# v's split first, k's hi halves ahead, and lasting k_lo buffers in a stick-breaking attention block

## The chip, the cores and the metric

The kernel runs on one core of one Trainium2 chip. The metric is the device time of one execution in microseconds (us). Everything is computed in fp32: a number is held as two parts, hi (the value rounded to fp32r) and lo (the rest), and a product of two such numbers takes three matmuls on TensorE (PE): hi by hi, lo by hi and hi by lo. The other engines are ScalarE (ACT), VectorE (DVE), GpSimd (POOL) and the queue that issues most DMAs (SP). Each engine works through its own list of instructions in order, and the engines wait for each other by semaphores.

## What is computed

One layer of a decoder trunk over 1024 tokens and a model width of 1024. The part that matters here is the attention: q, k and v come from one projection, q and k are normalised per head, and the weights are made by stick breaking.

```python
hn = rms_norm(h, norm1_g[i])
proj = hn @ w_in[i]
a_b, a_c, a_h, q, k, v, c_u, c_v = jnp.split(proj, split_idx, axis=-1)
...
q = rms_norm(q.reshape(bsz, s_len, ATTN_HEADS, HEAD_DIM), q_norm_g[i])
k = rms_norm(k.reshape(bsz, s_len, ATTN_HEADS, HEAD_DIM), k_norm_g[i])
y_b = stick_breaking_attention(q, k, v).reshape(bsz, s_len, ATTN_W)
...
h = h + jnp.concatenate([y_a, y_b, y_c], axis=-1) @ w_out[i]
f = jnp.square(jax.nn.relu(rms_norm(h, norm2_g[i]) @ w_ff1[i]))
h = h + f @ w_ff2[i]
gate = jax.nn.sigmoid(rms_norm(h, norm3_g[i]) @ w_ple_gate[i])
h = h + gate * (p[i] @ w_ple_proj[i])
```

In the attention, with z the scaled product of a query and a key (8 heads of 64), a weight is sigmoid(z) times the product of sigmoid(-z) over the later keys before the query, and the output is the weighted sum of v.

## The kernel before

The program runs in stages: the gating heads' projections and the first pair's q, k, v (up to about 100 us of the trace); attention, woven with the projections of the next pair of heads and at last with the convolution (to about 345 us); the output projection, the MLP and the last gate (to the end).

**The projection.** `project(pr)` (L343) makes q, k and v of one pair of heads, for four pairs. It goes over eight blocks of 128 tokens. A block is 24 matmuls (L165 to L167) into one PSUM bank `qkv_ps` of 128 x 384: q and k of two heads in columns 0 to 255, v in columns 256 to 383. Two banks (`ps_mm`, two buffers) serve in turn, so block b+2 can't begin before block b's bank has been read for the last time. I count the blocks through the four pairs, 0 to 31.

What reads a bank, in the order of the code: ACT squares q and k (`qk_sq`, L371), DVE sums the squares (`ss`, L374), POOL raises them to -1/2 (`rs`, L174), DVE multiplies q and k by that (`qk`, L379), and then v is split: ACT writes its hi part (`V`, L141) and DVE its lo part (`V`, L142). Where the reader of a bank changes from one engine to another, the built program has the second engine wait for the first.

**The turned bank.** After every second block `turn_qk` (L390) transposes q and k of two blocks on PE into a bank `qk_tr`, and for each of the two heads of the pair (64 partitions each) writes five parts from it: ACT q's hi (`QS`, L402) and k's hi (`KH`, L403) in the head's own rows, DVE q's lo (`QS`, L404, in the other rows) and k's lo (`KL`, L406), and ACT k's hi once more in the other rows (`KH`, L408). The other rows of `KL` have to be zero, and POOL clears them (L359) when a tile is taken, twice for each half of the tokens: 16 times.

**The attention.** `stick` (L427) makes z (L439, L441, L445) in two banks; ACT writes two sigmoids of it (`rem`, L446, and `wt`, L447); DVE runs the product over the later keys (L451, a scan), and POOL or DVE multiplies (L454). `gather` (L461) transposes the weights (`w_tr`, L476), splits them (`wT_hi` on ACT, `wT_lo` on DVE) and multiplies by V (`av`, L494).

**What sets the order.** `weave` (L267) alternates between attention and projection by units of PE work. Within that, a scheduler orders the instructions of each engine when the program is built, from costs of its own; the order on each engine is then fixed. Tiles of the tag `slot` come from one pool of 56, and `load_w` (L145) splits the next pair's weights (`whi` on ACT, `wlo` on DVE or POOL) in the same stretch.

## Time and profile before

| | us |
|---|---|
| time, median of 3 runs | 1219.47 |
| lowest and highest run | 1216.49, 1220.53 |
| the profiled execution's own time | 1217.19 |
| its span in the trace | 1215.2 |

The profile lists busy time by engine; a view by windows gives the busy time of each engine in a stretch of the span; a view of waits sums, for each engine and line, how long the engine stood idle and which instruction of another engine ended that; the timeline lists instructions in order of time, with the idle time just before one in brackets. PE is matmul and PEld the load of weights beside it. A matmul's listed time overlaps that of its neighbours, so the distance between two starts, not the listed time, is what it takes of PE.

### The profile page before, as it was taken

The page shows a single profiled execution, that of the slowest core. Times are in us where ns is not written, and L with a number is a line of the kernel's source. Part 1 is how long each engine was busy: PE and PEld are TensorE (multiplying, and loading weights), DVE is VectorE, ACT ScalarE, POOL GpSimd, SP SyncE. Part 2 cuts the span into 40 slices and gives each one's busy share as a digit, 9 for nine tenths or more (in the row PEclk, how much of TensorE's full clock was granted, in tenths as well). Part 3 has the DMA queues.
Part 4 walks back from the last instruction along what each step waited for, and adds up shares of the span by engine and source line. Part 5 has one row for each costly group of instructions (what it writes and reads, how often), then busy time and mean ns, then how long its engine had stood idle before and what let it go on. Part 6 is the DMA issues. An engine that isn't in the chain of part 4 may idle for free.

```text
span 1215.2 us, 17769 instructions
## 1 busy us (share of the span) xinstructions
PE 1188.7 (98%) x5852; PEld 1015.5 (84%) x5852; DVE 885.7 (73%) x1302; ACT 641.6 (53%) x1284; POOL 400.5 (33%) x408
## 2 busy tenths in 40 slices
PE   8999999999999999999999999999999999999997
PEld 7899999898878888888888888888888888888886
DVE  7846888888787757877877777787665557753597
ACT  7737777777654355743334343355443444546542
POOL 2324456465342312124553544421023301013412
PEclk9999999999999999999999999999999999999999
DMA  9703359898653786779989989778889985654857
GB/s 300 239 18 102 115 175 278 233 197 160 145 116 79 166 286 194 207 194 266 258 242 271 239 246 264 210 255 273 320 248 314 278 264 170 216 165 108 185 158 208
DMA packets 127964, 254.04 MB, mean 209 GB/s; under 512 B 14496, under 2 KB 22432, under 8 KB 127168
## 3 DMA queue, kind: packets, MB, share of 16 engines
q1 hardware_dynamic: 94992, 168.08, 41.7%
q0 software_dynamic: 27664, 57.05, 25.3%
q10 hardware_dynamic: 5216, 27.79, 6.3%
q8 instruction: 46, 0.75, 0.3%
q14 instruction: 46, 0.38, 0.1%
HBM read 192.30 MB, written 92.80 MB: 235 GB/s over the span
## 4 chain that ended last, share of the span: by engine, by line
PE 84%; DVE 6%; DMA 3%; ACT 3%; issue 2%; POOL 1%; ACTq 0%; SPq 0%; DVEq 0%; POOLq 0%
PE f_ps L811 25%; PE d_ps L811 25%; PE g_ps L811 6%; PE qkv_ps L165 3%; PE qkv_ps L167 3%; PE qkv_ps L166 3%; PE av L494 2%; PE w_tr L476 2%; DVE rem L451 2%; PE vu_ps L167 1%; PE vu_ps L165 1%; PE vu_ps L166 1%; PE o_ps L167 1%; PE o_ps L165 1%; PE o_ps L166 1%
## 5 line engine op out<-in xcount | busy, mean ns | idle before, releaser
L139 DVE TENSOR_TENSOR w_lo<-raw,w_hi 128x512 fp32r<-128x512 f32 x280 | 241.4, 865 | 87.0 <-ACT w_hi L138 85.1
L138 ACT CAST w_hi<-raw 128x512 fp32r<-128x512 f32 x280 | 171.9, 619 | 231.5 <-PE d_ps L811 114.0
L811 PE MATMUL f_ps<-hn_hi,w_hi 128*128 128x512 f32 x448 | 175.2, 392 | 0.0
L811 PE MATMUL f_ps<-hn_hi,w_lo 128*128 128x512 f32 x448 | 174.8, 391 | 0.0
L811 PE MATMUL f_ps<-hn_lo,w_hi 128*128 128x512 f32 x448 | 174.8, 390 | 0.0
L811 PE MATMUL d_ps<-f_hi,w_hi 128*128 128x512 f32 x448 | 174.8, 390 | 0.0
L811 PE MATMUL d_ps<-f_hi,w_lo 128*128 128x512 f32 x448 | 174.3, 389 | 0.0
L811 PE MATMUL d_ps<-f_lo,w_hi 128*128 128x512 f32 x448 | 174.3, 389 | 0.0
L451 DVE TENSOR_TENSOR_SCAN rem<-rem 128x128 f32<-128x128 f32 (+3 forms) x64 | 87.6, 1376 | 19.5 <-ACT rem L446 18.8
L811 PEld LDWEIGHTS f_ps<-hn_lo,w_hi 128*128 128x128 f32 x448 | 84.5, 189 | 17.9 <-issue 0.2
L811 PEld LDWEIGHTS f_ps<-hn_hi,w_hi 128*128 128x128 f32 x448 | 84.5, 189 | 17.9 <-issue 0.2
L811 PEld LDWEIGHTS f_ps<-hn_hi,w_lo 128*128 128x128 f32 x448 | 84.4, 188 | 17.6
L811 PEld LDWEIGHTS d_ps<-f_lo,w_hi 128*128 128x128 f32 x448 | 84.1, 188 | 17.6 <-issue 0.2
L811 PEld LDWEIGHTS d_ps<-f_hi,w_lo 128*128 128x128 f32 x448 | 84.1, 188 | 17.6
L811 PEld LDWEIGHTS d_ps<-f_hi,w_hi 128*128 128x128 f32 x448 | 84.1, 188 | 17.6 <-issue 0.2
L165 PE MATMUL qkv_ps<-whi,xn_hi 128*128 128x384 f32 x256 | 89.6, 350 | 6.8 <-DVE V L142 6.8
L166 PE MATMUL qkv_ps<-wlo,xn_hi 128*128 128x384 f32 x256 | 86.7, 339 | 0.0
L167 PE MATMUL qkv_ps<-whi,xn_lo 128*128 128x384 f32 x256 | 86.6, 338 | 0.0
L139 DVE TENSOR_TENSOR f_lo<-raw,f_hi 128x512 fp32r<-128x512 f32 x112 | 78.1, 728 | 10.1 <-ACT f_hi L138 9.9
L138 ACT CAST f_hi<-raw 128x512 fp32r<-128x512 f32 x112 | 67.1, 620 | 26.0 <-DMA raw<-f_dram 20.9
L797 POOL TENSOR_TENSOR S<-S,sq 128x512 f32<-128x512 f32 x19 | 25.6, 1345 | 160.2 <-ACT sq L873 160.2
L174 POOL TENSOR_TENSOR rs<-ss,mhalf 128x4 f32<-128x4 f32 x32 | 47.5, 1484 | 68.1 <-DVE ss L374 67.3
(247 smaller groups left out, 2707.9 us busy)
## 6 DMA issues: line engine op xcount, KB each, us to landing
raw<-in_w_ff SPq DMA_DIRECT2D x148, 256.0 KB, 4.1
raw<-f_dram SPq DMA_DIRECT2D x112, 256.0 KB, 5.1
raw<-w_sums SPq DMA_DIRECT2D x64, 256.0 KB, 3.7
f_dram<-f SPq DMA_DIRECT2D x48, 256.0 KB, 4.1
f_dram<-t SPq DMA_DIRECT2D x48, 256.0 KB, 3.7
w_sums<-in_w_ff POOLq DMA_DIRECT2D x8, 1024.0 KB, 12.2
w_sums<-w_sums POOLq DMA_DIRECT2D x8, 1024.0 KB, 12.4
raw<-in_w_out SPq DMA_DIRECT2D x28, 256.0 KB, 3.7
```

What stands on the lines that cost most here:

```text
L138: last_hi[0] = nc.scalar.copy(hi, src)
L139: low.tensor_tensor(out=lo, in0=src, in1=hi, op=ALU.subtract)
L165: nc.tensor.matmul(ps, lh, rh, start=first and i == 0, stop=False)
L166: nc.tensor.matmul(ps, lh, rl, start=False, stop=False)
L167: done = nc.tensor.matmul(ps, ll, rh, start=False, stop=last and i == len(terms) - 1)
L174: last_power[0] = nc.gpsimd.tensor_tensor(out=out, in0=in_, in1=mhalf[:, :n], op=ALU.pow)
L451: nc.vector.tensor_tensor_scan(out=back, data0=back, data1=back, initial=1.0, op0=ALU.mult, op1=ALU.bypass)
L476: nc.tensor.transpose(tr[:, n:n + P], wts[i][:, kb * P:(kb + 1) * P], ident)
L494: nc.tensor.matmul(av[:, first * P:], lhs, part[:, o:o + m], start=kb == 0 and part is hi, stop=kb == 2 * g + 1 and part is lo)
L797: return eng.tensor_tensor(out=out, in0=x, in1=y, op=ALU.add)
L811: done = nc.tensor.matmul(bank, l, r, start=first and k == 0 and i == 0, stop=k == len(b) - 1 and i == 2, skip_group_check=True)
```

## The change

The diff has three parts. In `project`, the split of v stands ahead of the squares instead of behind the product `qk`, so a bank is read by ACT (V hi), DVE (V lo), ACT (`qk_sq`), [DVE, POOL,] DVE (`qk`), and `qk` is the last reader instead of V lo. In `turn_qk`, ACT writes k's hi into the own and then the other rows right away, and DVE's two follow, so that ACT's three parts of a head stand together. And k's lo parts lie in lasting tiles, three for the first head of a pair and four for the second, whose other rows are cleared once: 7 clears instead of 16.

```diff
+    k_lo = [[None] * (3 + hh) for hh in range(2)]
+
+    def k_lo_tile(hh, i):
+
+        if k_lo[hh][i] is None:
+            t = k_lo[hh][i] = slot("k_lo", F32R)
+            nc.gpsimd.memset(t[(hi_p, lo_p)[hh]].bitcast(F32), 0.0)
+        return k_lo[hh][i]
+
     def project(pr):
...
             if t % 4 == 0:
-                for hh, other in enumerate((hi_p, lo_p)):
-                    KL[hh][th] = slot("KL", F32R)
-                    nc.gpsimd.memset(KL[hh][th][other].bitcast(F32), 0.0)
                 for hh in range(2):
+                    KL[hh][th] = k_lo_tile(hh, (2 * pr + th) % (3 + hh))
                     QS[hh][th] = slot("QS", F32R)
                     KH[hh][th] = slot("KH", F32R)
             ps = bank(ps_mm, "qkv_ps")[:, :384]
...
                 yield 18
+            if t % 2 == 0:
+                V[t // 2] = slot("V", F32R, (P, 2, 2, 2, HD))
+            v = V[t // 2][:, t % 2]
+            split(ps[:, 256:].rearrange("p (h d) -> p h d", d=HD), v[:, :, 0], v[:, :, 1], scale=r1[t])
 
             sq = half_tmp("qk_sq", (P, 4, HD + 1))
...
                 in1=rs.unsqueeze(2).broadcast_to([P, 4, HD]), op=ALU.mult)
-            if t % 2 == 0:
-                V[t // 2] = slot("V", F32R, (P, 2, 2, 2, HD))
-            v = V[t // 2][:, t % 2]
-            split(ps[:, 256:].rearrange("p (h d) -> p h d", d=HD), v[:, :, 0], v[:, :, 1], scale=r1[t])
...
             nc.scalar.activation(QS[hh][th][own, ws], q, AF.Copy, scale=gq[own])
-            nc.scalar.activation(KH[hh][th][own, ws], k, AF.Copy, scale=gk[own])
+            for part in (own, other):
+                nc.scalar.activation(KH[hh][th][part, ws], k, AF.Copy, scale=gk[own])
             nc.vector.scalar_tensor_tensor(out=QS[hh][th][other, ws], in0=q, scalar=gq[own],
                                            in1=QS[hh][th][own, ws], op0=ALU.mult, op1=ALU.subtract)
             nc.vector.scalar_tensor_tensor(out=KL[hh][th][own, ws], in0=k, scalar=gk[own],
                                            in1=KH[hh][th][own, ws], op0=ALU.mult, op1=ALU.subtract)
-            nc.scalar.activation(KH[hh][th][other, ws], k, AF.Copy, scale=gk[own])
```

The scheduler orders everything anew from the first of these instructions on; from the output projection on, the orders of before and of the change agree but for small exchanges.

The first place is on ACT at the end of the first pair. `qkv_ps_1251` is the bank of block 6, `qkv_ps_1323` that of block 7, and `z_1486` and `z_1492` are products that PE makes behind block 7. Before, the squares of block 6 stand ahead of the sigmoids of an earlier z, and the last reader that ACT gives (V hi) follows the turned bank's parts:

```order
L371 ACTIVATE qk_sq_1311<-qkv_ps_1251 128x4x64
L446 ACTIVATE rem_1373<-z_1375 128x384
...
L408 ACTIVATE KH_1161<-qk_tr_1296,c_gk 64x256
L402 ACTIVATE QS_1162<-qk_tr_1296,c_gq 64x256
L403 ACTIVATE KH_1163<-qk_tr_1296,c_gk 64x256
L141 ACTIVATE V_1320<-qkv_ps_1251,r_731 128x2x64
L138 CAST whi_1415<-stage_1413 128x384
L371 ACTIVATE qk_sq_1348<-qkv_ps_1323 128x4x64
```

With the change the same stretch of ACT reads:

```order
L409 ACTIVATE QS_1162<-qk_tr_1296,c_gq 64x256
L411 ACTIVATE KH_1163<-qk_tr_1296,c_gk 64x256 x2
L141 ACTIVATE V_1311<-qkv_ps_1251,r_731 128x2x64
L138 CAST whi_1409<-stage_1407 128x384
L141 ACTIVATE V_1311<-qkv_ps_1323,r_731 128x2x64
L138 CAST whi_1415<-stage_1413 128x384
L453 ACTIVATE rem_1484<-z_1492 128x512
L453 ACTIVATE rem_1484<-z_1486 128x128
L382 ACTIVATE qk_sq_1314<-qkv_ps_1251 128x4x64
L138 CAST whi_1421<-stage_1419 128x384
L382 ACTIVATE qk_sq_1350<-qkv_ps_1323 128x4x64
```

The squares of block 6 have moved from ahead of the turned bank's parts to behind the V of block 7 and the sigmoids of two products that PE makes after block 7.

On DVE behind that, with the change, the product `qk` of block 6 (the bank's last reader) stands behind these rows; `rem_1484` is the scan over the two sigmoids above, and the `wlo` are weights of the next pair:

```order
L458 SCALAR_TENSOR_TENSOR rem_1484<-rem_1484 128x640
L385 TENSOR_REDUCE ss_1317<-qk_sq_1314 128x4
L385 TENSOR_REDUCE ss_1353<-qk_sq_1350 128x4
L139 TENSOR_TENSOR wlo_1428<-stage_1425,whi_1427 128x384
L139 TENSOR_TENSOR wlo_2251<-stage_2248,whi_2250 128x384
L390 TENSOR_TENSOR qk_1321<-qkv_ps_1251,rs_1319 128x256
```

Before, the scan `rem_1484` stood behind both readers of block 6's bank; now it stands ahead of the sum of its squares.

The second place is on DVE in the third pair, for the bank of block 18 (`qkv_ps_2505` before). Before, from the sum of squares to the last reader, V lo:

```order
L374 TENSOR_REDUCE ss_2603<-qk_sq_2600 128x4
...
L451 SCALAR_TENSOR_TENSOR rem_2512<-rem_2512 128x1024
L454 TENSOR_TENSOR wt_2513<-wt_2513,rem_2512 128x1023
L379 TENSOR_TENSOR qk_2607<-qkv_ps_2505,rs_2605 128x256
...
L451 SCALAR_TENSOR_TENSOR rem_2621<-rem_2621 128x896
...
L142 SCALAR_TENSOR_TENSOR V_2609<-qkv_ps_2505,r_569,V_2609 128x2x64
```

With the change, where that bank is `qkv_ps_2499` and block 19's is `qkv_ps_2606`:

```order
L142 SCALAR_TENSOR_TENSOR V_2594<-qkv_ps_2499,r_569,V_2594 128x2x64
L142 SCALAR_TENSOR_TENSOR V_2594<-qkv_ps_2606,r_569,V_2594 128x2x64
L139 TENSOR_TENSOR wT_lo_2688<-w_tr_2682,wT_hi_2687 128x512
L458 SCALAR_TENSOR_TENSOR rem_2751<-rem_2751 128x640
L385 TENSOR_REDUCE ss_2600<-qk_sq_2597 128x4
L139 TENSOR_TENSOR wT_lo_2721<-w_tr_2716,wT_hi_2720 128x384
L385 TENSOR_REDUCE ss_2696<-qk_sq_2693 128x4
L458 SCALAR_TENSOR_TENSOR rem_2772<-rem_2772 128x768
L461 TENSOR_TENSOR wt_2773<-wt_2773,rem_2772 128x767
L390 TENSOR_TENSOR qk_2604<-qkv_ps_2499,rs_2602 128x256
```

Here too the sum of squares of the earlier block has moved behind a reader of the later block's bank, and two scans stand between V lo and the last reader.

## The prediction

> **What bounds the kernel now.** I read the page's busy times first, then windows by stage, then the waits of PE, then the timeline where PE waited longest.

> ```profile
> span 1215.2 us, 17769 instructions
> PE 1188.7 (98%) x5852; PEld 1015.5 (84%) x5852; DVE 885.7 (73%) x1302; ACT 641.6 (53%) x1284; POOL 400.5 (33%) x408
> ```

> PE is busy for 98% of the span, so a change to ACT, DVE and POOL alone can win at most what PE idles, and can lose by making it idle more. The windows, with the columns PE, PEld, DVE, ACT and POOL busy, tell where that is:

> ```profile
> 120.00:190.00 70.00, 68.81 (x455) 66.44 (x455) 60.41 (x90) 53.48 (x140) 36.07 (x34) 1.00 0.54 156
> 190.00:255.00 65.00, 61.27 (x405) 58.12 (x405) 55.77 (x86) 49.36 (x126) 36.97 (x33) 1.00 0.91 240
> 255.00:320.00 65.00, 61.58 (x400) 58.33 (x399) 56.40 (x88) 48.01 (x123) 33.15 (x32) 1.00 0.81 157
> 320.00:350.00 30.00, 26.93 (x138) 21.99 (x137) 18.87 (x25) 17.90 (x42) 8.72 (x9) 0.94 0.80 170
> ```

> From 120 to 320 us, where projection and attention are woven, PE idles 200 - 191.66 = 8.3 us, and from 320 to 350, where only the convolution is left to fill, 3.1. DVE is at 86% in the three windows to 320 (172.58 of 200) and ACT at 75% (150.85): with in-order lists there is little room behind a late instruction. The two longest sums among PE's waits from 80 to 350 us (us in total, times, longest):

> ```profile
> PE qkv_ps L165 <- DVE V L142: 6.8, 6, 2.5
> PE z L439 <- ACT wt L447: 2.7, 4, 1.0
> ```

> More than half of the idle time is six waits of a projection block for its bank, each ended by the split of v on DVE, the bank's last reader; the rest, 8.3 + 3.1 - 6.8 = 4.6 us at least, is above all attention waiting for ACT or DVE, as the z of the second row. The three longest of the six, at block 8, block 20 and block 28 (the column in brackets is the idle time):

> ```profile
> 118.64 0.44 PE L165 MATMUL qkv_ps<-whi,xn_hi 128*128 128x384 f32 x1 [1.20 <-DVE V L142]
> 215.12 0.44 PE L165 MATMUL qkv_ps<-whi,xn_hi 128*128 128x384 f32 x1 [1.61 <-DVE V L142]
> 282.67 0.44 PE L165 MATMUL qkv_ps<-whi,xn_hi 128*128 128x384 f32 x1 [2.54 <-DVE V L142]
> ```

> The other three make 6.8 - 5.35 = 1.45 us. So the bank's chain of readers is the place where this change decides.

> **The change part by part.** *V first.* The readers of a bank and their lengths:

> ```profile
> L371 ACT ACTIVATE qk_sq<-qkv_ps 128x256 f32<-128x256 f32 x32 | 12.6, 394 | 9.0 <-PE qkv_ps L167 8.6
> L374 DVE TENSOR_REDUCE ss<-qk_sq 128x4 f32<-128x260 f32 x32 | 13.2, 412 | 2.3 <-ACT qk_sq L371 2.0
> L174 POOL TENSOR_TENSOR rs<-ss,mhalf x32: 999/1048/3186, 82.5 to 316.9; 128x4 f32<-128x4 f32 x32
> L379 DVE TENSOR_TENSOR qk<-qkv_ps,rs 128x256 f32<-128x256 f32 x32 | 13.3, 417 | 12.2 <-POOL rs L174 12.1
> L141 ACT ACTIVATE V<-qkv_ps,r 128x128 fp32r<-128x128 f32 x32 | 11.8, 370 | 21.3 <-DVE qk L379 20.9
> L142 DVE SCALAR_TENSOR_TENSOR V<-qkv_ps,r,V 128x128 fp32r<-128x128 f32 x32 | 11.0, 343 | 2.9 <-ACT V L141 2.6
> ```

> Before, these run in this order, with five changes of engine: 0.39 + 0.41 + 1.05 + 0.42 + 0.37 + 0.34 = 2.98 us. The change puts the last two first; the sum is the same 2.98 us, and the changes of engine are again five (ACT, DVE, ACT, DVE, POOL, DVE). A bank isn't freed earlier by itself. What changes is who stands idle: ACT no longer idles 20.9 us behind `qk`; it now waits for V lo ahead of the squares, 0.34 us and a handover, times 32 at most 11 us. And what the end of the chain is queued behind changes: formerly ACT's list behind `qk`, now DVE's list behind `rs`.

> I went through the new order at the blocks where a bank is late, taking each row at its length, from the end of the matmuls of the block between (block b+1, for the bank that block b+2 needs). Lengths besides those above:

> ```profile
> L138 ACT CAST whi<-stage 128x384 fp32r<-128x384 f32 x31 | 15.7, 522 | 1.8 <-PE cv_ps L166 1.7
> L446 ACT ACTIVATE rem<-z 128x512 f32<-128x512 f32 x42 | 25.7, 611 | 8.1 <-PE z L441 5.9 <-PE z L445 1.8
> L446 ACT ACTIVATE rem<-z 128x128 f32<-128x128 f32 x14 | 3.9, 277 | 0.2 <-PE z L445 0.2
> L138 ACT CAST wT_hi<-w_tr 128x512 fp32r<-128x512 f32 x39 | 23.0, 596 | 2.8 <-PE w_tr L476 2.5
> L451 DVE TENSOR_TENSOR_SCAN rem<-rem 128x640 f32<-128x640 f32 x7 | 10.8, 1548 | 0.3
> L451 DVE TENSOR_TENSOR_SCAN rem<-rem 128x768 f32<-128x768 f32 x7 | 12.7, 1815 | 0.9 <-ACT rem L446 0.8
> L451 DVE TENSOR_TENSOR_SCAN rem<-rem 128x384 f32<-128x384 f32 x7 | 6.7, 959 | 2.5 <-ACT rem L446 2.4
> L451 DVE TENSOR_TENSOR_SCAN rem<-rem 128x256 f32<-128x256 f32 x7 | 4.7, 672 | 0.0
> L451 DVE TENSOR_TENSOR_SCAN rem<-rem 128x128 f32<-128x128 f32 x7 | 2.9, 412 | 1.2 <-ACT rem L446 1.2
> L139 DVE TENSOR_TENSOR wlo<-stage,whi 128x384 fp32r<-128x384 f32 x20 | 14.4, 733 | 0.9 <-ACT whi L138 0.8
> L139 DVE TENSOR_TENSOR wT_lo<-w_tr,wT_hi 128x384 fp32r<-128x384 f32 x26 | 14.2, 545 | 4.3 <-ACT wT_hi L138 4.3
> L454 DVE TENSOR_TENSOR wt<-wt,rem 128x767 f32<-128x767 f32 x7 | 6.7, 951 | 0.4
> ```

> For PE's own work in between I need the distance of matmuls by width; this stretch ahead of block 20 has both sizes:

> ```profile
> 211.65 0.82 PE L476 MATMUL w_tr<-ident,wt 128*128 128x128 f32 x6
> 212.22 0.48 PE L439 MATMUL z<-KH,QS 128*128 128x512 f32 x1
> 212.54 0.40 PE L441 MATMUL z<-KL,QS 128*128 128x512 f32 x1
> 212.77 0.22 PE L445 MATMUL z<-below,ident 128*128 128x128 f32 x1
> ```

> Six of 128 columns take 0.57 us, about 0.09 each; one of 512 takes 0.23 (212.54 to 212.77); I take 0.12 for 256 and 0.17 for 384.

> *Block 8 (bank of block 6).* By the rows shown of the change, ACT does V of block 7 (it can't start before block 7 ends), `whi`, two sigmoids, and the squares of block 6: 0.37 + 0.52 + 0.61 + 0.28 + 0.39 = 2.17. DVE's scan of 640 starts after both sigmoids, at 1.78, and ends at 3.33; the sum of squares ends at 3.74, `rs` at 4.79. But two `wlo` and block 7's sum stand ahead of `qk` on DVE, 0.41 + 0.73 + 0.73, to 5.61; with `qk` 6.03. PE has five products of z to do meanwhile (two of 512, three of 128: 0.73). It waits 5.3 us, against 1.20: **+4.1**.

> *Block 20 (bank of block 18).* V of block 19, `wT_hi`, two sigmoids: 1.86; scan of 640 to 3.41; sum 3.82; `wT_lo` 4.36; the next sum 4.77; scan of 768 to 6.59; `wt` 7.54; `qk` 7.96. PE's work in between in the new order is 12 of 128, 16 of 256, 2 of 384 and 6 of 512: 4.7. Wait 3.3, against 1.61: **+1.7**.

> *Block 28 (bank of block 26).* V of block 27, `wT_hi`, the squares and a sigmoid: 0.37 + 0.60 + 0.39 + 0.61 = 1.97; then on DVE a scan of 1024 (2.29, its row stands below), a `wT_lo` of 512, a sum, a product of 1023 and `qk`: with 0.7 and 1.2 for the second and the fourth, estimated by width from the rows of 384 and 767, it ends at 7.0. PE has 4.4 of work (19 of 128, 11 of 256, 6 of 512): 2.6, against 2.54: **0**.

> *Blocks 24 and 16*, which waited for no bank before. Ahead of block 24, V hi and V lo of block 23 are followed on DVE by scans of 128 and 256, a `wlo`, a `wT_lo`, a sum, a scan of 384 and `qk` of block 22: 0.37 + 0.34 + 0.41 + 0.67 + 0.73 + 0.55 + 0.41 + 0.96 + 0.42 = 4.9, with 3.4 of PE's work. Ahead of block 16, a `wT_lo`, a scan of 384, a `wlo` and `qk` of block 14 follow: 3.4, and 0.2 for handovers, with 2.7 of PE's work: **+1.5** and **+0.9**.

> *The other three bank waits* (1.45) end in places where the new order has PE's work longer than the rows: **-1.4**.

> *The turned bank.*

> ```profile
> ACT KH L408 <- DVE KL L406: 12.1, 12, 2.0
> ```

> The same ten instructions as before; the changes of engine fall from four to three, and the 12 waits of ACT for the other-row part fall to those between the two heads. DVE's first part starts one ACT part (0.46) later. With V first it gives ACT room, which reaches PE only through the 4.6 us that attention waits: between 0 and -4.6, and I take **-1.8**, two fifths, since DVE, not ACT, is the fuller engine.

> *The lasting tiles.* Nine clears on POOL go:

> ```profile
> L359 POOL MEMSET KL<- 64x512 f32 x15 | 7.8, 520 | 5.5 <-DMA y_dram<-y_both 4.8
> ```

> 9 x 0.52 = 4.7 us of an engine that idles more than 40% here, and up to 4.8 us of waits for a store whose tile they took over. No view names the clears as what anyone waited for, so nothing; if one stood ahead of an `rs` on the path, up to 3 us. A write into a lasting tile must wait for its last reader; with three tiles the first head's comes back in the second half of the next pair's projection, behind the last of its products in the program: nothing too.

> Sum: 4.1 + 1.7 + 0 + 1.5 + 0.9 - 1.4 - 1.8 = **+5.0 us**. The profiled execution took 1217.2 us, 2.3 under the median; so 1222.2 beside it, and **1224.5** on the scale of the median of 1219.5.

> **The rivals.** *Faster: ACT's list was the delay.* At block 28 `qk` had ended at 278.88, yet the bank came free at 282.6:

> ```profile
> 278.46 0.42 DVE L379 TENSOR_TENSOR qk<-qkv_ps,rs 128x256 f32<-128x256 f32 x1
> 279.90 0.47 ACT L408 ACTIVATE KH<-qk_tr,c_gk 64x256 fp32r<-64x256 f32 x1 [1.99 <-DVE KL L406]
> 282.27 0.35 DVE L142 SCALAR_TENSOR_TENSOR V<-qkv_ps,r,V 128x128 fp32r<-128x128 f32 x1
> ```

> If `qk` keeps its time, all six waits go and a part of the attention's: -6.8 - 2 = -9, so 1210 on the median's scale. It decides whether the squares run as soon as their block ends; in the rows on block 6 they run behind block 7. Against it, those rows. Chance 0.23.

> *No change.* A wait of PE lets ACT and DVE catch up, and what they catch up shortens the next wait; +4.1 at block 8 is then paid back by the blocks behind it. 1219.5, within 0.3% (3.7 us, about what a measurement can tell here). For it: DVE's lists are full, so some of the delay is only moved. Chance 0.27.

> *POOL's `rs` held by scans.* The row of `rs` above runs from 1.0 to 3.2 us; the longest lie beside scans:

> ```profile
> 274.93 2.29 DVE L451 TENSOR_TENSOR_SCAN rem<-rem 128x1024 f32<-128x1024 f32 x1
> 275.25 2.79 POOL L174 TENSOR_TENSOR rs<-ss,mhalf 128x4 f32<-128x4 f32 x1
> ```

> The new order puts a scan between the sum and `qk` at blocks 16 and 24, 0.96 us long; if `rs` starts only behind it, both waits grow by 0.8: 1226.1, and with the same at other blocks up to 1232. [...] Chance 0.10, and 0.40 for the forecast itself.

> **How the numbers follow.** Slower by over 0.3%: 0.40 + 0.10 = 0.50; within: 0.27; faster: 0.23. The faster case spreads from 1216 down to its full price at 1210 and a little beyond, of which a tenth is left out; above, the forecast without the -1.8 and the -1.4 is 1227.7, and with `rs` held at every block 1232 to 1236, of which the last tenth is left out: 1210 to 1234.

> **What would show it.** Right, if PE's wait at block 8 is some 5 us and is ended by `qk` on DVE, if the waits for `qkv_ps` sum to over 12 us, and ACT's wait for `qk` is gone from its list. The lasting tiles are right if no wait names `k_lo`. Wrong, if the waits for banks sum to under 5 us, or if the time differs behind 350 us, where the orders agree.

## The result and the profile after

Over four runs each, the changed kernel took 1235.66 us (median; 1233.41 to 1237.89) and the kernel before 1219.12 us: a ratio of 1.0143, with a 95% interval of 1.0122 to 1.0164. It is 16.5 us slower. The forecast, 1224.5, had the direction; the time lies 1.7 us above its range.

The page of the changed kernel, span and busy times:

```profile
span 1232.3 us, 17759 instructions
## 1 busy us (share of the span) xinstructions
PE 1195.1 (97%) x5852; PEld 1022.5 (83%) x5852; DVE 881.3 (72%) x1302; ACT 640.6 (52%) x1284; POOL 398.6 (32%) x399
```

The span grew by 17.1 us. PE's idle time (span less busy) grew from 26.5 to 37.2, by 10.7, and PE's busy time by 6.4 for the same 5852 matmuls. The first is waits; the second needs a reason of its own. The windows (PE, PEld, DVE, ACT, POOL busy, then granted clock, DMA share and GB/s) show both:

```profile
120.00:190.00 70.00, 64.23 (x415) 62.04 (x415) 52.57 (x84) 48.16 (x126) 31.93 (x28) 0.95 0.45 132
190.00:255.00 65.00, 54.88 (x323) 51.80 (x324) 49.09 (x67) 39.28 (x101) 26.72 (x22) 0.92 0.83 217
255.00:320.00 65.00, 59.00 (x365) 55.58 (x364) 52.24 (x72) 44.33 (x116) 31.98 (x31) 0.95 0.88 176
320.00:350.00 30.00, 29.58 (x187) 26.93 (x186) 25.31 (x49) 21.82 (x57) 12.00 (x14) 1.00 0.38 92
```

In the first three, PE idles 5.8, 10.1 and 6.0 us (before: 1.2, 3.7 and 3.4), and the granted clock, 1.00 before in all three, is 0.92 to 0.95. DVE and ACT do less in them too: nobody is overloaded, work comes too late. Now PE's waits from 80 to 350 us (total, times, longest). First those of the kernel before that the prediction did not list, then the changed kernel's:

```profile
PE av L494 <- ACT y_both L503: 1.0, 1, 1.0
PE av L494 <- DVE wT_lo L139: 1.0, 1, 1.0
PE av L494 <- DVE y_b L512: 0.9, 1, 0.9
```

```profile
PE qk_tr L405 <- DVE qk L390: 6.8, 3, 5.1
PE qkv_ps L165 <- DVE qk L390: 4.6, 4, 2.0
PE av L501 <- DVE wT_lo L139: 4.0, 3, 2.9
PE av L501 <- ACT wT_hi L138: 3.7, 2, 3.5
PE z L446 <- ACT wt L454: 2.2, 4, 1.0
PE av L501 <- ACT y_both L510: 2.2, 2, 1.8
PE w_tr L483 <- DVE wt L461: 1.6, 1, 1.6
PE cv_ps L165 <- DVE qk L390: 0.4, 1, 0.4
```

Waits ended by a bank's last reader were 6.8 us and are 11.8 (the three lines with `qk`), 5.0 more. Those inside attention were 5.6 and are 13.7, 8.1 more. The projection ends much later, by the last group of its matmuls before and with the change:

```profile
L167 PE MATMUL qkv_ps<-whi,xn_lo x2: 336/341/346, 313.5 to 314.0; 128*128 128x384 f32 x2
```

```profile
L167 PE MATMUL qkv_ps<-whi,xn_lo x2: 336/341/346, 339.3 to 339.8; 128*128 128x384 f32 x2
```

26 us later; in return less attention and convolution is left behind 350 us, and PE idles 8.1 us there (882.0 - 873.9) against 10.2 before.

**Where it begins.** ACT around block 6, whose matmuls end at 110.6 before and 111.1 with the change. Before (start, length, engine, line):

```profile
110.58 0.38 ACT L371 ACTIVATE qk_sq<-qkv_ps 128x256 f32<-128x256 f32 x1 [0.41 <-PE qkv_ps L167]
...
116.72 0.46 ACT L403 ACTIVATE KH<-qk_tr,c_gk 64x256 fp32r<-64x256 f32 x1
117.20 0.37 ACT L141 ACTIVATE V<-qkv_ps,r 128x128 fp32r<-128x128 f32 x1
```

With the change:

```profile
116.02 0.94 ACT L411 ACTIVATE KH<-qk_tr,c_gk 64x256 fp32r<-64x256 f32 x2
116.99 0.37 ACT L141 ACTIVATE V<-qkv_ps,r 128x128 fp32r<-128x128 f32 x1
...
117.66 0.37 ACT L141 ACTIVATE V<-qkv_ps,r 128x128 fp32r<-128x128 f32 x1
...
118.32 0.77 ACT L453 ACTIVATE rem<-z 128x512 f32<-128x512 f32 x2
118.97 0.40 ACT L382 ACTIVATE qk_sq<-qkv_ps 128x256 f32<-128x256 f32 x1
```

V hi runs at 117.2 before and at 117.0 now, both times right behind a k hi part of the turned bank: putting it first in the code did not bring it forward. But the squares, which formerly ran at once, at 110.58, now stand behind it, at 118.97. Formerly the chain of four instructions on three engines, from the squares to `qk`, ran while V hi waited; now it only starts then:

```profile
119.22 1.48 DVE L458 TENSOR_TENSOR_SCAN rem<-rem 128x640 f32<-128x640 f32 x1
...
120.62 0.72 DVE L385 TENSOR_REDUCE ss<-qk_sq 128x4 f32<-128x260 f32 x2
...
121.46 2.30 POOL L174 TENSOR_TENSOR rs<-ss,mhalf 128x4 f32<-128x4 f32 x2
...
122.81 0.42 DVE L390 TENSOR_TENSOR qk<-qkv_ps,rs 128x256 f32<-128x256 f32 x1
123.29 0.69 PE L405 MATMUL qk_tr<-ident,qk 128*128 128x128 f32 x2 [5.12 <-DVE qk L390]
```

PE waits 5.12 us, at the transposes that need this `qk` and stand just ahead of block 8's matmuls, which need its bank.

**What follows a long wait.** Windows over that place:

```profile
117.00:120.40 3.40, 1.17 (x8) 0.93 (x6) 3.35 (x6) 3.40 (x10) 1.93 (x3) 1.00 0.46 135
120.40:123.70 3.30, 0.41 (x3) 0.41 (x3) 2.49 (x6) 1.17 (x5) 3.30 (x3) 0.51 0.60 199
123.70:127.20 3.50, 3.50 (x13) 3.50 (x12) 0.42 (x1) 0.00 (x0) 1.03 (x2) 0.50 0.48 137
127.20:131.00 3.80, 3.80 (x25) 3.73 (x25) 1.25 (x3) 2.44 (x6) 1.32 (x1) 0.99 0.00 0
```

For 3.5 us behind the wait, PE runs at half its clock (granted 0.50): 13 matmuls where the next 3.8 us hold 25 (matmuls of 384 columns start 0.32 us apart in it and 0.17 behind it). Between 100 us and the last matmul, the trace's record of the granted clock has 0.50 only in lengths of 3.41 us or, once, 6.83. They come to two spells of 3.41 us before (at 339.2 and 527.0) and to seven with the change (from 120.5, twice the length, and from 192.1, 212.6, 233.1, 274.1 and 311.6).

### The profile page after: what moved, and what is told of

Its sections match the earlier page's. It is cut to its first block, busy times and chain, and to the rows that moved or that the text cites. A ratio compares the mean times of both kernels' runs of the same rounds, so it can differ in the third digit from the quotient of the medians.

```text
span 1232.3 us, 17759 instructions
## 1 busy us (share of the span) xinstructions
PE 1195.1 (97%) x5852; PEld 1022.5 (83%) x5852; DVE 881.3 (72%) x1302; ACT 640.6 (52%) x1284; POOL 398.6 (32%) x399
## 4 chain that ended last, share of the span: by engine, by line
PE 81%; DVE 3%; ACT 3%; DMA 2%; issue 1%; POOL 1%; ACTq 0%; DVEq 0%; POOLq 0%
PE f_ps L818 25%; PE d_ps L818 25%; PE g_ps L818 6%; PE o_ps L165 2%; PE o_ps L167 2%; PE o_ps L166 2%; PE qkv_ps L165 2%; PE av L501 2%; PE qkv_ps L166 2%; PE qkv_ps L167 2%; PE cv_ps L165 2%; PE cv_ps L167 2%; PE w_tr L483 2%; PE cv_ps L166 2%; DMA y_both<-y_both 2%
## 5 line engine op out<-in xcount | busy, mean ns | idle before, releaser
L139 DVE TENSOR_TENSOR w_lo<-raw,w_hi 128x512 fp32r<-128x512 f32 x280 | 244.3, 876 | 85.8 <-ACT w_hi L138 81.9
L138 ACT CAST w_hi<-raw 128x512 fp32r<-128x512 f32 x280 | 172.0, 619 | 234.6 <-PE d_ps L818 112.7
L458 DVE TENSOR_TENSOR_SCAN rem<-rem 128x128 f32<-128x128 f32 (+3 forms) x64 | 90.8, 1423 | 14.0 <-ACT rem L453 13.6
L165 PE MATMUL qkv_ps<-whi,xn_hi 128*128 128x384 f32 x256 | 93.0, 363 | 4.6 <-DVE qk L390 4.6
L166 PE MATMUL qkv_ps<-wlo,xn_hi 128*128 128x384 f32 x256 | 88.5, 346 | 0.0
L167 PE MATMUL qkv_ps<-whi,xn_lo 128*128 128x384 f32 x256 | 88.3, 345 | 0.0
L139 DVE TENSOR_TENSOR f_lo<-raw,f_hi 128x512 fp32r<-128x512 f32 x112 | 77.1, 718 | 13.0 <-ACT f_hi L138 12.3
L138 ACT CAST f_hi<-raw 128x512 fp32r<-128x512 f32 x112 | 67.1, 620 | 28.7 <-DMA raw<-f_dram 24.0
L461 POOL TENSOR_TENSOR wt<-wt,rem 128x127 f32<-128x127 f32 (+4 forms) x40 | 45.0, 1139 | 101.1 <-DVE rem L458 65.3
```

The costliest lines, as they stand in the source:

```text
L138: last_hi[0] = nc.scalar.copy(hi, src)
L139: low.tensor_tensor(out=lo, in0=src, in1=hi, op=ALU.subtract)
L165: nc.tensor.matmul(ps, lh, rh, start=first and i == 0, stop=False)
L166: nc.tensor.matmul(ps, lh, rl, start=False, stop=False)
L167: done = nc.tensor.matmul(ps, ll, rh, start=False, stop=last and i == len(terms) - 1)
L458: nc.vector.tensor_tensor_scan(out=back, data0=back, data1=back, initial=1.0, op0=ALU.mult, op1=ALU.bypass)
```

## The experiments

Theory A was, at first: V first makes squares and `qk` late, and that is the loss. Rivals were B (the turned bank's order), C (any edit reshuffles the built order at a cost) and D (the lasting tiles wait for old readers). Ratios are to the kernel before on the same chip, with 95% intervals.

**1. V first alone.**

```diff
             ps = bank(ps_mm, "qkv_ps")[:, :384]
...
+            split(ps[:, 256:].rearrange("p (h d) -> p h d", d=HD), v[:, :, 0], v[:, :, 1], scale=r1[t])
             sq = half_tmp("qk_sq", (P, 4, HD + 1))
...
-            split(ps[:, 256:].rearrange("p (h d) -> p h d", d=HD), v[:, :, 0], v[:, :, 1], scale=r1[t])
```

> The kernel before with V first alone. Theory A (V first puts the squares behind other ScalarE work and the product qk behind scans, so a bank is given back late): slower by 12 to 18 us, PE's waits for qkv_ps and qk_tr ended by qk on DVE sum to over 10 us from 80 to 360 us, and the granted clock from 190 to 255 us is again below 1.00. Rival B (the turned bank's order pushes late parts into attention's way): within 3 us of before. Rival C (any edit there reshuffles the built order, and each costs several us): slower by 4 to 10 us, as the other two edits alone would be.

1230.5 us, ratio 1.0113 (1.0085 to 1.0141). PE's waits ended by `qk` sum to 11.7 us (6.0 and 5.7), the granted clock from 190 to 255 us is 0.97, and five half-clock spells stand in the record. As theory A has it.

**2. The turned bank's order alone.**

```diff
-            nc.scalar.activation(KH[hh][th][own, ws], k, AF.Copy, scale=gk[own])
+            for part in (own, other):
+                nc.scalar.activation(KH[hh][th][part, ws], k, AF.Copy, scale=gk[own])
...
-            nc.scalar.activation(KH[hh][th][other, ws], k, AF.Copy, scale=gk[own])
```

> The kernel before with the turned bank's order alone. Theory A: within 3 us of before, and V lo on DVE still ends the bank waits. Rival B: slower by 10 us or more. Rival C: slower by 4 to 10 us.

1210.72 us, ratio 0.9942 (0.9923 to 0.9961): 7 us faster, which none of the three had. PE's bank waits on V lo fall from 6.8 to 2.9 us and the waits of z from 2.7 to 0.2; new are 3.5 us in which `w_tr` waits for the turned bank's `KL`.

**3. The lasting tiles alone.**

```diff
-                    KL[hh][th] = slot("KL", F32R)
-                    nc.gpsimd.memset(KL[hh][th][other].bitcast(F32), 0.0)
+                    KL[hh][th] = k_lo_tile(hh, (2 * pr + th) % (3 + hh))
```

> The kernel before with the lasting tiles of k's lo parts alone. Theory A: within 2 us of before, and no wait of DVE or PE names k_lo for over 0.5 us. Rival D (the first write into a lasting tile waits for its last reader, two pairs back): slower by over 5 us with waits named k_lo. Rival C: slower by 4 to 10 us.

1218.53 us, ratio 1.0010 (0.9993 to 1.0027): no difference that shows. Rivals C and D fall.

**4. The turned bank's order and the lasting tiles**, that is the changed kernel with V put back behind `qk` (the diffs of 2 and 3 together).

> The changed kernel with V put back behind qk, so the turned bank's order and the lasting tiles together. Theory A: within 4 us of before, 12 us or more under the changed kernel. Rivals B and D: within 5 us of the changed kernel. Rival C: slower than before by 8 us or more, with none of the three to blame.

1214.36 us, ratio 0.9970 (0.9952 to 0.9987). So V first, on top of these two, costs 1.0143 / 0.9970 = 1.017, some 21 us. It is the whole loss. The parts don't add up one by one: alone, V first costs 12 us (experiment 1), and where it stands, the other two win nothing (1235.66 us with them, 1230.5 without; the intervals of the two ratios overlap).

**5. The price of a wait by itself.** Behind the last matmul:

```diff
+    def timed_waits(rounds, copies, filler):
+        t = late_slot("w", "tw", F32R)
+        nc.vector.tensor_copy(t, below.bitcast(F32).unsqueeze(1).broadcast_to([P, 4, P]))
+        for _ in range(rounds):
+            burst = late_bank("burst")
+            for _ in range(32):
+                nc.tensor.matmul(burst, ident_r, t, start=True, stop=True)
+            if filler:
+                other = late_bank("filler")
+                for _ in range(filler):
+                    nc.tensor.matmul(other, ident_r, t, start=True, stop=True)
+            x = late_slot("tmp", "tx")
+            nc.vector.tensor_copy(x, burst)
+            for _ in range(copies):
+                y = late_slot("tmp", "tx")
+                nc.vector.tensor_copy(y, x)
+                x = y
+            t = late_slot("w", "tw", F32R)
+            nc.vector.tensor_copy(t, x)
+    for copies, filler in ((0, 0), (1, 0), (2, 0), (3, 0), (5, 0), (8, 0), (5, 10), (8, 16)):
+        timed_waits(8, copies, filler)
```

> The kernel before, and behind its last matmul 64 rounds that add nothing to the output: a burst of 32 matmuls of 512 columns, then a chain of VectorE copies that the next burst waits for. Sections of 8 rounds with 0, 1, 2, 3, 5 and 8 extra copies, then 5 and 8 again with 10 and 16 matmuls beside the chain that wait for nothing. Theory K (an idle stretch of about 1.6 to 1.8 us or more in one of TensorE's 3.41 us windows halves the granted clock for the next 3.41 us): a burst stands at 7 to 7.4 us where the wait is under 1.5 us, and takes up to 1.7 us longer where it is over 3.4 us, in nearly every round; the two sections with filling matmuls go back to the short burst at the same chain. Rival L (the halved clock only accompanies other trouble): the burst has one length in all sections, and a round is burst plus wait.

Its windows, one for each section of eight rounds (those with 0, 2, 3, 5 and 8 extra copies, then 5 and 8 with filling matmuls):

```profile
1207.43:1279.43 72.00, 61.71 (x259) 47.40 (x257) 13.07 (x27) 0.84 (x2) 0.57 (x1) 1.00 0.03 12
...
1355.23:1436.29 81.06, 63.39 (x256) 48.63 (x256) 16.12 (x33) 0.00 (x0) 0.00 (x0) 0.98 0.00 0
1436.29:1528.36 92.07, 70.71 (x256) 54.02 (x257) 19.53 (x41) 0.00 (x0) 0.00 (x0) 0.89 0.00 0
1528.36:1635.61 107.25, 78.50 (x256) 59.88 (x257) 26.36 (x57) 0.00 (x0) 0.00 (x0) 0.79 0.00 0
1635.61:1752.68 117.07, 77.26 (x256) 59.16 (x256) 36.60 (x81) 0.00 (x0) 0.00 (x0) 0.82 0.00 0
1752.68:1845.08 92.40, 82.28 (x337) 63.92 (x337) 26.38 (x57) 0.00 (x0) 0.00 (x0) 0.98 0.00 1
1845.08:1941.50 96.42, 87.97 (x369) 68.80 (x370) 31.76 (x70) 0.00 (x0) 0.00 (x0) 1.00 0.00 0
```

Two bursts of the section with 2 copies, from the timeline (the bracket is PE's wait ahead of the burst):

```profile
1394.84 9.26 PE L1288 MATMUL burst<-tw,ident 128*128 128x512 f32 x32 [2.17 <-DVE tw L1300]
1406.26 7.73 PE L1288 MATMUL burst<-tw,ident 128*128 128x512 f32 x32 [2.17 <-DVE tw L1300]
```

The chain between two bursts takes 1.24, 1.71, 2.17, 2.63, 3.55 and 4.94 us in the six sections. Up to 1.71 every burst takes 7.7 us; behind 2.17 one of eight takes 1.5 more, behind 2.63 six of eight do, and behind 3.55 and 4.94 each takes 1.3 to 2.8 more (the expectation had 7 to 7.4 us and at most 1.7 more; the granted clocks of these two sections, 0.79 and 0.82, come to some 13 and 12 spells of 3.41 us in eight rounds, so some waits have two behind them). With matmuls that fill the same chains of 3.55 and 4.94, the bursts are back at 7.73, all but the first, which still follows an unfilled wait; a round with 5 copies falls from 107.25 / 8 = 13.4 to 92.40 / 8 = 11.6 us. Theory K holds, with a point between 1.7 and 2.6 us of wait (the last section has it closer); rival L falls.

**6. The changed kernel with the squares first.** Theory A is now split. A1: V lo's turn on DVE ahead of the squares is the delay. A2: it is `qk` as the last reader.

```diff
-            split(ps[:, 256:].rearrange("p (h d) -> p h d", d=HD), v[:, :, 0], v[:, :, 1], scale=r1[t])
             sq = half_tmp("qk_sq", (P, 4, HD + 1))
...
                                  AF.Square, scale=HD ** -0.5)
+            vs = ps[:, 256:].rearrange("p (h d) -> p h d", d=HD)
+            nc.scalar.activation(v[:, :, 0], vs, AF.Copy, scale=r1[t])
+            nc.vector.scalar_tensor_tensor(out=v[:, :, 1], in0=vs, scalar=r1[t], in1=v[:, :, 0],
+                                           op0=ALU.mult, op1=ALU.subtract)
```

> The changed kernel with the squares put ahead of v's two parts: ScalarE squares, V hi, VectorE V lo, sum, rs, qk. Theory A1 (V lo on VectorE stands between V hi and the squares, so squares and then qk come late): back to 1211 to 1218 us. Theory A2 (qk as the bank's last reader, behind rs in VectorE's list, is what costs): 1226 us or more, with PE's waits still ended by qk.

1209.4 us, ratio 0.9929 (0.9911 to 0.9947), 26 us under the changed kernel, though `qk` is still the bank's last reader. A2 falls. Over blocks 5 to 29 the squares start 0.9 us behind the end of their block on average, against 4.8 in the changed kernel and 1.0 before.

**7. The changed kernel with V hi first and V lo last.**

```diff
-            split(ps[:, 256:].rearrange("p (h d) -> p h d", d=HD), v[:, :, 0], v[:, :, 1], scale=r1[t])
+            vs = ps[:, 256:].rearrange("p (h d) -> p h d", d=HD)
+            nc.scalar.activation(v[:, :, 0], vs, AF.Copy, scale=r1[t])
             sq = half_tmp("qk_sq", (P, 4, HD + 1))
...
                 in1=rs.unsqueeze(2).broadcast_to([P, 4, HD]), op=ALU.mult)
+            nc.vector.scalar_tensor_tensor(out=v[:, :, 1], in0=vs, scalar=r1[t], in1=v[:, :, 0],
+                                           op0=ALU.mult, op1=ALU.subtract)
```

> The changed kernel with V hi first and V lo last: ScalarE V hi, squares, VectorE sum, GpSimd rs, VectorE qk, V lo. The bank passes once from ScalarE to VectorE. Theory A1 and A2 both: 1208 to 1217 us, PE's bank waits ended by V lo on VectorE. If instead any work put ahead of the squares is the cost (A3): 1224 us or more.

1220.96 us, ratio 1.0031 (1.0019 to 1.0042): between the expectations, and 11.6 us above experiment 6. V hi alone ahead of the squares costs that much, with V lo out of the way, so A1 isn't enough. In eight of the 25 blocks the squares start over 3 us late, each time just behind their own V hi.

**8. V hi right behind the squares, V lo last**, on the kernel before with the turned bank's new order.

```diff
                                  AF.Square, scale=HD ** -0.5)
+            vs = ps[:, 256:].rearrange("p (h d) -> p h d", d=HD)
+            nc.scalar.activation(v[:, :, 0], vs, AF.Copy, scale=r1[t])
...
                 in1=rs.unsqueeze(2).broadcast_to([P, 4, HD]), op=ALU.mult)
-            split(ps[:, 256:].rearrange("p (h d) -> p h d", d=HD), v[:, :, 0], v[:, :, 1], scale=r1[t])
+            nc.vector.scalar_tensor_tensor(out=v[:, :, 1], in0=vs, scalar=r1[t], in1=v[:, :, 0],
+                                           op0=ALU.mult, op1=ALU.subtract)
```

> The kernel before with the turned bank's order, and V hi moved from behind qk to right behind the squares, V lo staying last: the bank passes once from ScalarE to VectorE. A1 and A2: 1204 to 1212 us, the fastest so far if ScalarE's wait for qk ever ended a bank wait; one half-rate spell at most before 350 us. A3: also no loss. If V hi's place doesn't matter: 1210 to 1212 us, as the turned bank's order alone.

1208.59 us, ratio 0.9930 (0.9915 to 0.9945), inside experiment 2's interval: V hi's place behind the squares is worth little by itself. One half-clock spell stands before 350 us; the expectation had one at most.

**9. The changed kernel with the turned bank issued one step later.** Theory A3: the squares are late because they now follow V hi, and the built order puts V hi of some blocks behind the turned bank's parts.

```diff
-                later(72, lambda t=t, qk=qk: turn_qk(heads[pr], t, qk))
+                later(73, lambda t=t, qk=qk: turn_qk(heads[pr], t, qk))
```

> The changed kernel with the turned bank's work issued one step later (73 units behind qk in place of 72), so that V first of the next block stands ahead of it in the program. Theory A3 (the squares are late because V hi, which they now follow, is itself late: in the changed kernel V hi of blocks 6, 10, 14, 18, 22, 26 and 30 runs right behind the turned bank's last part on ScalarE): the squares start under 2 us behind their block's end on average (4.8 in the changed kernel), PE's waits ended by qk fall under 4 us, time 1208 to 1218 us. Theory A1 (V lo's turn on VectorE ahead of the squares is the delay, wherever V hi stands): the squares start over 3.5 us late, 1226 us or more.

1212.28 us, ratio 0.9937 (0.9915 to 0.9959): this one number takes the loss away. A1's 1226 us or more falls. The squares still start 3.9 us late on average over blocks 5 to 29 (V hi: 1.5, against 2.7), and the waits ended by `qk` are 4.9 us, not under 4, so both of A3's bounds on delay were missed. But the average hides where: in the seven blocks that A3 names, V hi starts 0.6 us behind the end of its block in place of 7.3, and the squares 2.6 in place of 9.5; in the other blocks the squares start 4.4 us late, later than the 3.3 of the changed kernel. That fits A3. `qk` also has a step longer until the transposes need it; this run doesn't part the two.

**10. Experiment 6 without the lasting tiles.**

```diff
-                    KL[hh][th] = k_lo_tile(hh, (2 * pr + th) % (3 + hh))
+                    KL[hh][th] = slot("KL", F32R)
+                    nc.gpsimd.memset(KL[hh][th][other].bitcast(F32), 0.0)
```

> The order squares, V hi, V lo, sum, rs, qk with the turned bank's new order and the k lo tiles of before (so the sixth experiment without the lasting tiles). If the lasting tiles cost some 3 us there as beside the turned bank's order alone: 1204 to 1208 us. If they cost nothing or help there: 1209 us or more.

1209.56 us, ratio 0.9921 (0.9896 to 0.9945), like experiment 6: the tiles cost nothing there. Whether the 3 us between experiments 2 and 4 are theirs or the order's stays open.

**11. Experiment 8 with the turned bank one step later** (the diff of 9).

> The eighth experiment (squares, V hi, sum, rs, qk, V lo, turned bank's order, tiles of before) with the turned bank's work issued one step later. If V hi behind the turned bank still held a bank there: 1203 to 1207 us. If not: 1207 to 1211 us, or slower where the later turned bank makes attention wait for QS and KH (waits of z for QS or KH would show it).

1206.62 us, ratio 0.9904 (0.9877 to 0.9931), the lowest median: 12 us under the kernel before and 29 under the changed one. It lies in the first range, but its interval overlaps experiment 8's, so a gain from the later turned bank isn't shown. Its page:

```profile
span 1204.7 us, 17786 instructions
## 1 busy us (share of the span) xinstructions
PE 1185.2 (98%) x5852; PEld 1013.3 (84%) x5852; DVE 875.0 (73%) x1302; ACT 640.0 (53%) x1284; POOL 399.9 (33%) x408
```

PE has no half-clock spell before its last matmul, and its busy time, 1185.2, is the least of all.

**12. The changed kernel with the squares first in the blocks t = 2 and t = 6 of a pair alone.**

```diff
-            split(ps[:, 256:].rearrange("p (h d) -> p h d", d=HD), v[:, :, 0], v[:, :, 1], scale=r1[t])
+            if not (t % 4 == 2):
+                split(ps[:, 256:].rearrange("p (h d) -> p h d", d=HD), v[:, :, 0], v[:, :, 1], scale=r1[t])
...
                                  AF.Square, scale=HD ** -0.5)
+            if t % 4 == 2:
+                split(ps[:, 256:].rearrange("p (h d) -> p h d", d=HD), v[:, :, 0], v[:, :, 1], scale=r1[t])
```

> The changed kernel with the squares ahead of V in the blocks t = 2 and t = 6 of each pair alone (blocks 2, 6, 10, 14, 18, 22, 26, 30), V first in the others. Theory A3 (the loss comes from the blocks whose V hi the built order puts behind the turned bank's parts, which are these): most of the 25 us to the sixth experiment come back, 1209 to 1218 us. Theory A1 (V lo's turn on VectorE ahead of the squares costs in every block alike): a quarter comes back, 1226 to 1231 us.

1213.15 us, ratio 0.9951 (0.9933 to 0.9970). Eight of 32 blocks give back 22.5 of the 26 us. ACT at block 6, whose matmuls end at 111.7 here:

```profile
111.70 0.38 ACT L383 ACTIVATE qk_sq<-qkv_ps 128x256 f32<-128x256 f32 x1 [0.35 <-PE qkv_ps L167]
...
116.61 0.95 ACT L414 ACTIVATE KH<-qk_tr,c_gk 64x256 fp32r<-64x256 f32 x2
117.58 0.37 ACT L141 ACTIVATE V<-qkv_ps,r 128x128 fp32r<-128x128 f32 x1
```

And PE at the transposes of this block's `qk`:

```profile
119.35 0.44 PE L408 MATMUL qk_tr<-ident,qk 128*128 128x128 f32 x2 [0.60 <-DVE qk L393]
```

V hi stands where it stood, behind the turned bank; the squares run at once, and PE's 5.12 us shrink to 0.60.

**13. The complement: V first in those blocks alone, the squares first in the other 24.**

```diff
-            if not (t % 4 == 2):
+            if not (t % 4 != 2):
...
-            if t % 4 == 2:
+            if t % 4 != 2:
```

> The complement: V first in the blocks t = 2 and t = 6 alone, the squares first in the other 24. Theory A3: the loss stays, 1224 to 1236 us. Theory A1: three quarters come back, 1213 to 1218 us.

1240.75 us, ratio 1.0167 (1.0135 to 1.0198), above A3's own bound. Its busy times and PE's longest wait:

```profile
PE 1205.1 (97%) x5852; PEld 1029.0 (83%) x5852; DVE 882.6 (71%) x1302; ACT 641.2 (52%) x1284; POOL 389.9 (31%) x399
```

```profile
PE qk_tr L408 <- DVE qk L393: 7.5, 1, 7.5
```

Twelve half-clock spells of 3.41 us stand in its record, and PE is busy 20 us longer than in experiment 11 for the same matmuls. A3 holds: the loss comes from the blocks t = 2 and t = 6. In blocks 6, 10, 14, 18, 22, 26 and 30 the squares start 9.4 us late here and 0.1 in experiment 12 (9.5 in the changed kernel, 0.1 before); in the others from 5 to 29, 1.4 and 4.1. Averaged over blocks 5 to 29 the two runs hardly differ (3.4 and 3.2 us), and yet they lie 28 us apart. Each edit has everything ordered anew, so a few us between two runs may be that alone; it wasn't measured apart, but 28 us with this pattern are more. Why the scheduler puts V hi of just these behind the turned bank was not tried.

## Why the prediction was right or wrong, point by point

The sum was +5.0 us; the profiled execution has +17.1. By the prediction's steps:

**The bank waits: +6.8 forecast, +5.0 measured.** The mechanism was right: V first frees no bank earlier, the last reader is `qk`, behind DVE's list, and ACT's wait for `qk` is gone. Block 8 came out at 5.12 us against 5.3. The others were oversized or moved: block 20 has 1.99 against 3.3, block 28 0.59 against 2.6, block 24 0.62 against 1.5, and block 16 1.38 against 0.9. The forecast's five sum to 13.6 and these to 9.7; waits at transposes and before a convolution make up the 11.8. "The waits for `qkv_ps` sum to over 12" failed as it was put: 4.6 stand there and 6.8 at the turned bank that needs the same `qk`.

**The room that ACT gains: -1.8 forecast, +8.1 measured.** This is the step that failed. "With V first it gives ACT room, which reaches PE only through the 4.6 us that attention waits" took the two edits of ACT's list together. The turned bank's order alone does win (experiment 2, 7 us, more than the term), but beside V first it wins nothing (experiments 1 and 4): V first makes blocks late, and a late block stops the projection, whose last matmul comes 26 us later. PE's waits inside attention, for `wT_lo`, `wT_hi`, `wt` and `y_both`, grow from 5.6 to 13.7 us. (The 4.6 of the prediction was itself too low: it took the wait at block 8, which ends at 118.64, off the idle time behind 120 us.) In experiments 6, 8, 10 and 12, whose squares run at once in the blocks t = 2 and t = 6, these waits sum to 1.8, 1.8, 1.6 and 5.3 us, beside 5.3, 3.4, 4.1 and 0.8 in which `w_tr` waits for a part of the turned q and k. So they come with late blocks, but not in proportion: 8.6 us in experiment 1 and only 6.7 in experiment 13, the slowest. How a late block brings them about is not shown; that projection work is missing between the steps of attention is argued from the windows.

**The clock: not in the sum, +6.4 measured.** This step failed too: a wait was priced at its own length, and what follows it at nothing. By experiment 5 a wait of 2.6 us or more mostly has one or two half-clock spells behind it (2.63 us in six of eight rounds, 3.55 and 4.94 in each), and a spell full of matmuls, 0.32 us apart and not 0.17, costs some 3.41 / 2 = 1.7 us. Two spells of 3.41 us before and seven with the change are five more; at half speed, less the parts in which PE idled anyway, they are worth (23.9 - 3.8) / 2 - (6.8 - 0.3) / 2 = 6.8 us, beside the 6.4 that PE's busy time grew. The same holds across the runs: PE is busy 1185.2 us with no spell, 1188.7 with two, 1194.0 with five (experiment 1), 1195.1 with seven and 1205.1 with twelve (experiment 13), 1.4 to 1.8 each. In the traces a spell is a granted clock of 0.50 for 3.41 us or a multiple; how idle PE was ahead of one stands in the last section.

**The rest: 0 forecast, -2.4 measured**, mostly behind 350 us, where the prediction took the orders to agree: PE idles 2.1 us less there. So 5.0 + 8.1 + 6.4 - 2.4 = 17.1. A time that differs behind 350 us was one of the prediction's signs of being wrong, and it came.

**The lasting tiles: 0 forecast**, and ratios of 1.0010 (experiment 3) and 0.9921 against 0.9929 (10 and 6) agree. One wait of PE names `k_lo`, 0.2 us.

**The rivals.** "Faster" was said to hinge on whether the squares run as soon as their block ends. That was the right hinge: they don't in the changed kernel, and where they do (experiment 6, and experiment 12 in the eight blocks) it is 6 to 8 us faster than before. But that is no more than the 7 us of the turned bank's order alone; V's early place won nothing that shows. "No change" fell: of the 13 us that PE idles more up to 350 us, 2 come back later. The rival of `rs` held by scans was right in that `rs` ends behind a running scan (by 0.80 us or more, below), and its price was too high. Its row before and with the change:

```profile
L174 POOL TENSOR_TENSOR rs<-ss,mhalf 128x4 f32<-128x4 f32 x32 | 47.5, 1484 | 68.1 <-DVE ss L374 67.3 <-PE qkv_ps L165 0.8
```

```profile
L174 POOL TENSOR_TENSOR rs<-ss,mhalf 128x4 f32<-128x4 f32 x32 | 47.9, 1499 | 60.7 <-DVE ss L385 60.7
```

An `rs` that starts while a scan runs ends 0.80 us or more behind that scan, in all eleven such cases before and in all eleven with the change; one that starts ahead of the scan can take its 1.0 us beside it (1.01 at block 6 before, 1.03 at block 18 with the change). There are as many held as before, so the mean stays, 1484 and 1499 ns. At the two blocks that the rival named, `rs` did grow: from 1.05 to 1.69 us at block 14, with `qk` right behind it and PE's 1.38 us of wait behind that, and from 1.33 to 1.90 at block 22, where `qk` comes 3.9 us later anyway. That makes some 0.6 us of the 17.1 at most.

## What to carry to other kernels

Among the readers of a shared buffer, the one that starts a long chain over several engines belongs first, and a short one whose place is set by something else belongs where it can be late: ask of each moved instruction what holds it now, since what is put behind it inherits that delay. In experiment 5 the waits of TensorE of up to 1.71 us cost their length alone, and six of eight of 2.63 us and all of 3.55 us cost 1.3 us or more beyond it: price a long wait at its length and at least one half-clock spell (some 1.7 us) more, and a lone one below 1.7 us at its length. And try the parts of a change one by one and together: here one part alone won 7 us, another lost 12 alone and 21 beside the rest, and the order with the lowest median (experiment 11) has, beside the turned bank's new order, only a different place for V hi and a later step for the turned bank. Look at late blocks one by one, too: the average over all blocks hid which of them cost the time.

## What the runs showed of the hardware

One spell, between 517 and 555 us in nine of the fifteen runs, has no idle time of PE in the three windows ahead of it; what starts it isn't shown.
